# Row normalization on one core: ten-row tiles in five buffers, one whole-row descriptor per partition for each load and store, and two rows of each tile scaled on ScalarE

## The chip, the core and the metric

The kernel runs on one core of a Trainium2 chip. The metric is device time in microseconds (us): the median of 3 runs of the kernel before is 316.5 us (316.41 to 316.51).

## The reference

The input is a 32 x 512 x 1024 array in float32, 67.11 MB. Each row of 1024 values is divided by the sum of its absolute values:

```python
sums = np.sum(np.abs(x), axis=-1, keepdims=True)
return (x / (sums + 1e-8)).astype(np.float32)
```

Every value is read once and written once, 134.22 MB in all.

## The kernel before

The 16384 rows are spread over 128 partitions, 128 rows for each. A tile holds 12 rows per partition, 48 KB per partition and 6 MB in all; the last tile has 8. There are eleven tiles and four buffers (`BUFS = 4`). `piece` says which rows a tile takes: the first 32 rows of every partition (`HEAD`) form one block, which tiles 0, 1 and the last share, so that a partition's rows of these tiles lie in runs inside a block of 128 KB per partition; every other tile is one contiguous block with 48 KB per partition.

`load` (line 87) issues the load of a tile on SyncE's DMA queue, and `store` (line 97) the store on ScalarE's. `max_dma_last_dim` limits the bytes of one descriptor, that is of one contiguous run: `WHOLE` allows 48 KB (a partition's whole share of a tile is one run), `HALF` cuts it into two of 24 KB. Tiles 0 and 1 are loaded with 48 KB runs, all others in halves. The first tile is stored in two DMAs: its first three rows (`FIRST`) as runs of 4 KB, the other nine as runs of 36 KB. The third tile from the end is stored in two DMAs of six rows each; the last two are stored with whole runs; the others in halves. A DMA over 128 partitions is served by 16 DMA engines, 8 partitions on each.

`normalize` computes in place. VectorE sums the absolute values of all rows of the tile in one instruction (line 47), adds the small constant (line 54), takes the reciprocals (line 56) and multiplies most rows by them in one instruction (line 58). `split` names, for some tiles, how many rows go another way: `kt` rows are scaled on VectorE one at a time (line 65), `ks` rows on ScalarE one at a time (line 68). Before, ScalarE scales 4 rows of the first tile, 3 of the next two, 2 of the next to last and 4 of the last, 16 in all.

The order of instructions on each engine is the order of the program (a schedule by hand): four loads first, then for each tile its computation, its store, and the load of the tile that will use its buffer. SyncE's queue therefore holds a load until the store of the buffer's earlier tile has landed, and ScalarE's queue holds its own rows of each tile and then the tile's store.

Of the kernel before, what the change touches and what calls it, by code (L numbers as in the profile page):

```python
# [1 line left out]

# [4 lines left out]

FP32 = mybir.dt.float32
EPS = 1e-8


@with_exitstack
def kernel(
    ctx: ExitStack,
    tc: tile.TileContext,
    x: bass.AP,
    out: bass.AP,
):
    nc = tc.nc
    P = nc.NUM_PARTITIONS  # L20

    x_flat = x.flatten_outer_dims()
    out_flat = out.flatten_outer_dims()
    n, d = x_flat.shape

    R = 12
    BUFS = 4
    HEAD = 32
    per_partition = n // P
    assert n % P == 0 and (per_partition - HEAD) % R == 0  # L30
    rows = [R] * ((per_partition - HEAD) // R + 2) + [HEAD - 2 * R]

    def piece(flat, i):
        head = flat[: P * HEAD, :].rearrange("(p r) d -> p r d", p=P)
        if i < 2:
            return head[:, R * i : R * (i + 1), :]
        if i == len(rows) - 1:
            return head[:, 2 * R :, :]
        a = P * (HEAD + R * (i - 2))
        return flat[a : a + P * R, :].rearrange("(p r) d -> p r d", p=P)  # L40

    sbuf = ctx.enter_context(tc.tile_pool(name="sbuf", bufs=BUFS))
    stats = ctx.enter_context(tc.tile_pool(name="stats", bufs=len(rows)))

    def normalize(x_tile, k, kv, kt):
        s = stats.tile([P, R], FP32)
        nc.vector.tensor_reduce(  # L47
            out=s[:, :k],
            in_=x_tile[:, :k, :],
            axis=mybir.AxisListType.X,  # L50
            op=mybir.AluOpType.add,
            apply_absolute_value=True,
        )
        nc.vector.tensor_scalar_add(out=s[:, :k], in0=s[:, :k], scalar1=EPS)  # L54
        inv = stats.tile([P, R], FP32)
        nc.vector.reciprocal(out=inv[:, :k], in_=s[:, :k])  # L56
        if kv:
            nc.vector.tensor_mul(  # L58
                out=x_tile[:, :kv, :],
                in0=x_tile[:, :kv, :],  # L60
                in1=inv[:, :kv].unsqueeze(2).to_broadcast([P, kv, d]),
            )
        for r in range(kv, kv + kt):
            row = x_tile[:, r, :]
            nc.vector.tensor_scalar_mul(out=row, in0=row, scalar1=inv[:, r : r + 1])  # L65
        for r in range(kv + kt, k):
            row = x_tile[:, r, :]
            nc.scalar.activation(  # L68
                out=row,
                in_=row,  # L70
                func=mybir.ActivationFunctionType.Copy,
                scale=inv[:, r : r + 1],
            )

    last = len(rows) - 1
    split = {0: (3, 4), 1: (0, 3), 2: (0, 3), last - 1: (0, 2), last: (4, 4)}

    tiles = {}

    HALF, WHOLE = 24576, 49152
    FIRST = 3

    def load(i):
        x_tile = tiles[i] = sbuf.tile([P, R, d], FP32, name="x_tile")
        nc.sync.dma_start(out=x_tile[:, : rows[i], :], in_=piece(x_flat, i), max_dma_last_dim=WHOLE if i < 2 else HALF)  # L87

    def store(i):
        if i == 0:  # L90
            parts = [(0, FIRST, 4 * d), (FIRST, R, WHOLE)]
        elif i == last - 2:
            parts = [(0, R // 2, HALF), (R // 2, R, HALF)]
        else:
            parts = [(0, rows[i], WHOLE if i >= last - 1 else HALF)]
        for a, b, size in parts:
            nc.scalar.dma_start(
                out=piece(out_flat, i)[:, a:b, :],
                in_=tiles[i][:, a:b, :],
                max_dma_last_dim=size,  # L100
            )

    def compute(i):
        k = rows[i]
        kt, ks = split.get(i, (0, 0))
        normalize(tiles[i], k, k - kt - ks, kt)

    with tc.manual_schedule():
        for i in range(BUFS):
            load(i)  # L110
        for i in range(len(rows)):
            compute(i)
            store(i)
            if i + BUFS < len(rows):
                load(i + BUFS)


# [1 line left out]
_INS = ['x']  # L119
_OUTS = [((32, 512, 1024), 'float32')]  # L120


# [23 lines left out]
```

## Time and profile before

| What | Value |
|---|---|
| Median of 3 runs | 316.5 us (316.41 to 316.51) |
| Profiled execution: span from first to last instruction | 315.2 us |
| Profiled execution: time of its own beside the span | not listed; the runs lie 1.3 us above the span |
| VectorE (DVE) busy | 260.6 us, 83% of the span, 50 instructions |
| ScalarE (ACT) busy | 18.5 us, 6%, 17 instructions |
| Loads (queue q1) | 11 DMAs, 2736 packets, 67.11 MB |
| Stores (queue q10) | 13 DMAs, 3024 packets, 67.11 MB |
| Mean rate over the span | 426 GB/s |

The page cuts the span into 40 equal slices of 7.9 us. A digit is the busy share of a slice in tenths, 9 meaning 90% or more; for the DMA row it is the mean over the core's 16 DMA engines. Names such as `x_tile<-in_x_dram` are out<-in, and L47 is line 47 of the kernel. DVE is VectorE, ACT is ScalarE, SPq and ACTq are the sequencers of SyncE and ScalarE, which issue DMAs. In the chain and the timeline the first number is the start in us from the start of the span, the second the duration. A packet record in the trace is one descriptor: its queue, its start, its duration and its bytes; the small records of 4 bytes are the semaphore updates that each of the 16 engines makes at the end of a DMA.

### The profile page before, as it was taken

How to read it: one execution, taken by the hardware profiler on the slowest of the kernel's cores; microseconds unless marked ns; L12 is line 12 of the kernel's file. 1: busy time of each engine (PE TensorE's matmuls, PEld its weight loads, DVE VectorE, ACT ScalarE, POOL GpSimd, SP SyncE). 2: the span in 40 equal slices, each digit the busy share in tenths (PEclk: the TensorE clock that was granted, in tenths of full speed). 3: DMA queues.
4: the chain of work that ended last, by engine and by line, in shares of the span. 5: the costliest groups of instructions: out<-in, count | busy, mean ns of one | idle time of the engine just before them, and what ended most of it. 6: DMA issues, size and time to landing. Idle time of an engine off the chain costs nothing.

```text
span 315.2 us, 172 instructions
## 1 busy us (share of the span) xinstructions
DVE 260.6 (83%) x50; ACT 18.5 (6%) x17; POOL 0.2 (0%) x4
## 2 busy tenths in 40 slices
DVE  0079999999999999989996997999699969999000
ACT  0010503004000000000000000000000000203200
POOL 0000000000000000000000000000000000000000
DMA  8999999999999999999999999999999999999997
GB/s 318 480 399 412 437 407 464 411 436 413 415 446 437 415 446 437 415 449 434 415 449 437 412 449 437 412 449 437 415 446 437 415 437 434 432 428 496 399 408 324
DMA packets 5761, 134.22 MB, mean 426 GB/s; under 512 B 385, under 2 KB 385, under 8 KB 769
## 3 DMA queue, kind: packets, MB, share of 16 engines
q1 hardware_dynamic: 2736, 67.11, 49.8%
q10 hardware_dynamic: 3024, 67.11, 49.4%
q14 instruction: 1, 0.00, 0.0%
HBM read 67.11 MB, written 67.11 MB: 426 GB/s over the span
## 4 chain that ended last, share of the span: by engine, by line
DVE 40%; DMA 33%; another core or an unknown queue 18%; ACT 1%; issue 0%; SPq 0%
DVE s L47 23%; DMA x_tile<-in_x_dram 17%; DMA out_dram<-x_tile 16%; DVE x_tile L58 15%; ACT x_tile L68 1%; DVE x_tile L65 1%; DVE inv L56 0%; DVE s L54 0%; SPq L87 0%
## 5 line engine op out<-in xcount | busy, mean ns | idle before, releaser
L47 DVE TENSOR_REDUCE s<-x_tile 128x12 f32<-128x12288 f32 (+1 forms) x11 | 138.2, 12562 | 29.8 <-DMA x_tile<-in_x_dram 29.8
L58 DVE TENSOR_TENSOR x_tile<-x_tile,inv 128x12288 f32<-128x12288 f32 (+3 forms) x10 | 113.6, 11358 | 0.5
L68 ACT ACTIVATE x_tile<-x_tile,inv 128x1024 f32<-128x1024 f32 x16 | 17.2, 1138 | 256.9 <-DVE inv L56 256.9
L65 DVE TENSOR_SCALAR x_tile<-x_tile,inv 128x1024 f32<-128x1024 f32 x7 | 4.8, 749 | 0.0
L56 DVE RECIPROCAL inv<-s 128x12 f32<-128x12 f32 (+1 forms) x11 | 2.5, 226 | 0.4
L68 ACT ACT_TABLE_LOAD x1 | 1.3, 1283 | 17.8 <-DMA x_tile<-in_x_dram 17.8
L54 DVE TENSOR_SCALAR s<-s 128x12 f32<-128x12 f32 (+1 forms) x11 | 1.9, 174 | 0.4
L130 POOL MEMSET const-bfloat16-1.0<- 128x1 bf16 x1 | 0.1, 101 | 0.0
L130 POOL MEMSET const-uint8-127<- 128x1 uint8 x1 | 0.1, 101 | 0.0
L130 POOL MEMSET const-float32-0.0<- 128x1 f32 x1 | 0.1, 98 | 0.2 <-issue 0.2
L130 POOL MEMSET const-float32-1.0<- 128x1 f32 x1 | 0.1, 98 | 0.0
## 6 DMA issues: line engine op xcount, KB each, us to landing
x_tile<-in_x_dram SPq DMA_DIRECT2D x10, 6144.0 KB, 36.9
out_dram<-x_tile ACTq DMA_DIRECT2D x8, 6144.0 KB, 49.1
out_dram<-x_tile ACTq DMA_DIRECT2D x2, 3072.0 KB, 33.4
out_dram<-x_tile ACTq DMA_DIRECT2D x1, 4608.0 KB, 37.9
x_tile<-in_x_dram SPq DMA_DIRECT2D x1, 4096.0 KB, 32.2
out_dram<-x_tile ACTq DMA_DIRECT2D x1, 4096.0 KB, 20.9
out_dram<-x_tile ACTq DMA_DIRECT2D x1, 1536.0 KB, 29.3
```

The lines of the kernel that those rows point to most:

```text
L47: nc.vector.tensor_reduce(out=s[:, :k], in_=x_tile[:, :k, :], axis=mybir.AxisListType.X, op=mybir.AluOpType.add, apply_absolute_value=True,)
L54: nc.vector.tensor_scalar_add(out=s[:, :k], in0=s[:, :k], scalar1=EPS)
L56: nc.vector.reciprocal(out=inv[:, :k], in_=s[:, :k])
L58: nc.vector.tensor_mul(out=x_tile[:, :kv, :], in0=x_tile[:, :kv, :], in1=inv[:, :kv].unsqueeze(2).to_broadcast([P, kv, d]),)
L65: nc.vector.tensor_scalar_mul(out=row, in0=row, scalar1=inv[:, r : r + 1])
L68: nc.scalar.activation(out=row, in_=row, func=mybir.ActivationFunctionType.Copy, scale=inv[:, r : r + 1],)
L130: nc = _bacc.Bacc("TRN2", target_bir_lowering=False, num_devices=1)
```

## The change

A tile has ten rows per partition instead of twelve (40 KB per partition, 5 MB in all), and there are five buffers instead of four. The 128 rows of a partition make twelve tiles of ten rows and a last one of eight, thirteen in all. Every tile is one contiguous block; no block is shared. Each tile is loaded by one DMA and stored by one DMA without a limit on the run, so that a partition's share is one descriptor of 40 KB (32 KB for the last tile). ScalarE scales two rows of every tile, and four of the first and the last, as before in those two. The pool of the small statistics tiles has 26 buffers instead of 11.

```diff
-    R = 12
-    BUFS = 4
-    HEAD = 32
+    R = 10
+    BUFS = 5
     per_partition = n // P
-    assert n % P == 0 and (per_partition - HEAD) % R == 0
-    rows = [R] * ((per_partition - HEAD) // R + 2) + [HEAD - 2 * R]
+    assert n % P == 0
+    rows = [R] * (per_partition // R) + [per_partition % R]
 
     def piece(flat, i):
-        head = flat[: P * HEAD, :].rearrange("(p r) d -> p r d", p=P)
-        if i < 2:
-            return head[:, R * i : R * (i + 1), :]
-        if i == len(rows) - 1:
-            return head[:, 2 * R :, :]
-        a = P * (HEAD + R * (i - 2))
-        return flat[a : a + P * R, :].rearrange("(p r) d -> p r d", p=P)
+        a = P * R * i
+        return flat[a : a + P * rows[i], :].rearrange("(p r) d -> p r d", p=P)
...
-    stats = ctx.enter_context(tc.tile_pool(name="stats", bufs=len(rows)))
+    stats = ctx.enter_context(tc.tile_pool(name="stats", bufs=2 * len(rows)))
...
-    split = {0: (3, 4), 1: (0, 3), 2: (0, 3), last - 1: (0, 2), last: (4, 4)}
+    split = {0: (3, 4), last: (4, 4)}
...
-    HALF, WHOLE = 24576, 49152
-    FIRST = 3
-
     def load(i):
         x_tile = tiles[i] = sbuf.tile([P, R, d], FP32, name="x_tile")
-        nc.sync.dma_start(out=x_tile[:, : rows[i], :], in_=piece(x_flat, i), max_dma_last_dim=WHOLE if i < 2 else HALF)
+        nc.sync.dma_start(out=x_tile[:, : rows[i], :], in_=piece(x_flat, i))
 
     def store(i):
-        if i == 0:
-            parts = [(0, FIRST, 4 * d), (FIRST, R, WHOLE)]
-        elif i == last - 2:
-            parts = [(0, R // 2, HALF), (R // 2, R, HALF)]
-        else:
-            parts = [(0, rows[i], WHOLE if i >= last - 1 else HALF)]
-        for a, b, size in parts:
-            nc.scalar.dma_start(
-                out=piece(out_flat, i)[:, a:b, :],
-                in_=tiles[i][:, a:b, :],
-                max_dma_last_dim=size,
-            )
+        nc.scalar.dma_start(out=piece(out_flat, i), in_=tiles[i][:, : rows[i], :])
 
     def compute(i):
         k = rows[i]
-        kt, ks = split.get(i, (0, 0))
+        kt, ks = split.get(i, (0, 2))
         normalize(tiles[i], k, k - kt - ks, kt)
```

## The prediction

> **What bounds the kernel now.** I read the 40 slices first, then the queues, then the waits of the engines and of the DMA queue, then stretches and the tail of the chain. The 40 slices of the page (busy tenths; 9 is 90% or more):
>
> ```profile
> DVE  0079999999999999989996997999699969999000
> DMA  8999999999999999999999999999999999999997
> GB/s 318 480 399 412 437 407 464 411 436 413 415 446 437 415 446 437 415 449 434 415 449 437 412 449 437 412 449 437 415 446 437 415 437 434 432 428 496 399 408 324
> DMA packets 5761, 134.22 MB, mean 426 GB/s; under 512 B 385, under 2 KB 385, under 8 KB 769
> ```
>
> The DMA row has no hole between its first and last slice. VectorE is also dense, but it has holes, and what it waits for is the loads; ScalarE waits for VectorE, and SyncE's queue for the stores (columns: us in total, times, longest):
>
> ```profile
> ACT x_tile L68 <- DVE inv L56: 256.9, 5, 190.5
> DVE s L47 <- DMA x_tile<-in_x_dram: 29.8, 6, 17.8
> SPq L87 <- DMA out_dram<-x_tile: 242.1, 8, 63.3
> ```
>
> Stretches of the trace (us; busy time of DVE, ACT and POOL; clock; DMA share; GB/s) give the plateau and one dip:
>
> ```profile
> 60.00:65.00 5.00, 5.00 (x2) 0.00 (x0) 0.00 (x0) 1.00 1.01 387
> 90.00:250.00 160.00, 149.89 (x24) 0.00 (x0) 0.00 (x0) 1.00 1.00 433
> ```
>
> So the DMA engines set the end: share 1.00, 433 GB/s for 160 us. In the trace's packet records the first data packet starts at 1.73 us and the last ends at 313.83 us; between them each engine goes from packet to packet. Outside lie 1.7 us ahead and 1.3 us behind. The time is the sum of what each DMA engine pays per descriptor, as long as a queue has something for it.
>
> **What one descriptor costs.** The records have a size and a duration: 4 KB 159 ns, 24 KB 912 ns, 48 KB 1815 ns, alike for loads and stores. From 24 to 48 KB is 903 ns for 24 KB, which leaves 9 ns a descriptor. Successive records overlap: on one engine 48 KB packets start 1812 ns apart, and in the steady stretch SyncE issues a load every 29.08 us:
>
> ```profile
> 160.35 0.37 SPq L87
> ...
> 189.48 0.37 SPq L87
> ...
> 218.50 36.97 DMA x_tile<-in_x_dram
> ```
>
> One 12-row tile in and one out is 32 descriptors of 24 KB per engine: 29.08 / 32 = 909 ns. So a descriptor costs 903 ns per 24 KB and a fixed 6 ns by starts, 9 ns by records. I take 6, since starts make the elapsed time.
>
> **Descriptors before.** Each of 16 engines serves 8 partitions. Loads: 2 tiles x 8, then 8 x 16, then 16 for the last, 160. Stores: 24 + 8 for the first tile, 7 x 16, 2 x 8 (two halves), 8, 8, 176. That is 336; 336 x 16 + 24 DMAs x 16 semaphore records + 1 = 5761, the page's packets. **After:** 13 loads and 13 stores x 8 = 208. The removal of 128 is worth 128 x 6 ns = 0.77 us (9 ns: 1.15; nothing hidden: 0 is the other end). Checked as a sum: before 310.24 us (16 x 1812, 128 x 909, 16 x 608; stores 24 x 156.5, 8 x 1360.5, 128 x 909, 8 x 1210, 8 x 1812), after 192 x 1511 + 16 x 1210 = 309.47. The observed 312.1 us is 310.24 and: 0.74 for first packets (2.25 to 2.85 us where later ones take 1.815), 0.69 for slow 24 KB loads, 0.2 for semaphore records, 0.2 for spread between engines. The first packets stay. Two more DMAs add 2 x 9 ns of semaphore records.
>
> The **slow loads** are the dip at 60 to 65 us: one round of 16 loads took 1.15 to 1.60 us instead of 0.912, and some near 38 to 46 us a little more. Both fall where 24 KB loads alternate with the 4 KB store descriptors of the first tile; over the 160 us in which both sides have 24 KB there are none. The changed kernel has equal sizes from the first store on. No row shows 40 KB beside 40 KB: bounds are all 0.69 gone, and one such round more (+0.6). I take half gone, -0.35, since an accident cannot be told from a pattern with one instance.
>
> **What costs nothing, and its cover.** VectorE: by shape, 12949 ns for 12 rows and 8686 for 8 is 1066 ns a row to reduce; 10825 for ten rows and 9758 for nine is 1067 a row to scale. A middle tile is 10.82 + 0.4 + 8.69 = 19.9 us. DMA needs 2 x 8 x 1511 = 24.2 us for the same tile, so 4.2 us cover it; VectorE's sum falls from 260.6 to about 248 and is not seen. ScalarE gets 30 rows instead of 16 (1138 ns each); two take 2.3 us beside VectorE's 8.7. The store on ScalarE's queue waits for both engines, and behind it stands only the next tile's ScalarE rows, which wait for VectorE anyway. A fifth buffer and thirteen tiles: SyncE issues five loads at the start (26 MB, 60 us of DMA at 433); load 5 waits for store 0. That store is issued near 15 + 10.8 + 0.4 + 5.6 = 32 us and shares the engines until about 57, when loads 3 and 4 are still queued. Without that cover a queue would stand dry for the 1.0 us seen from issue (0.73) to first packet (1.73). More stats buffers take no time; SyncE and ScalarE issue 26 DMAs instead of 24 at about 0.37 us, beside the transfers.
>
> **The tail** must be worked out, for only it can open a hole. From about 34 us both queues are never empty, and the engines take descriptors in turn (in the records of 59 to 62 us, one load of 24 KB and one store of 4 KB alternate; from 255 to 275 us loads of 16 KB beside stores of 24 KB get 0.40 of the bytes, which is 16/40). Equal sizes give halves. By 34 us loads have moved (34 - 2.5) x 433 = 13.6 MB; the other 53.5 at 216 GB/s take 247 us: the last load lands near 282 to 284 us. The last tile is the same 8 rows as now:
>
> ```profile
> 279.79 8.70 DVE s L47
> ...
> 292.09 1.13 ACT x_tile L68
> ```
>
> From landing (279.77) to the store's issue (293.25) is 13.5 us, so the last store comes at 297 us. Then stores have moved 53.5 MB of 67.1 at 283; of 13.6 left, 9.4 to 8.4 MB precede the last, 19 to 22 us, to 302.7. Cover: about 5 us, less 1.0 for issue to first packet. Now it is 304 - 293; the change halves it but leaves it.
>
> **Sum:** -0.77 - 0.35 + 0.02 = -1.1 us. The span 315.2 becomes 314.1. The median of the runs, 316.5, lies 1.3 above the span (the profiled execution has no separate time beside the span); that rest is start and end, unchanged: **315.4 us**.
>
> **Rivals.** A measurement can tell about 0.2%, 0.63 us, from no change.
> 1. *Descriptors cost less than their start-to-start distance says*, and the slow round was chance: gain 0 to 0.6, middle 0.4 (3 ns each), 316.1. For it: 6 ns rests on two large differences. Against: records (9) and starts (6) agree in sign. A 0.6 us slow round eating the gain ends in the same place. Chance 0.24. The Trainium skill, page DMA: Bandwidth & Descriptors, section Why small descriptors are slow, gives a fixed overhead of about 3 cycles a packet against one per 32 bytes. As an estimate by that page, a 24 KB descriptor is 768 + 3 cycles and 128 fewer give 0.45 us, 316.05; the trace's 6 ns is nearly twice its 3.5.
> 2. *The tail runs dry, slower.* Place: between the next-to-last and the last store. If loads got less than half of the turns, the last load lands later and its store is due when no other is left. Share 0.49 shifts the landing by 5 us and spends the cover; 0.486 is the point from which the kernel is slower by 0.2%; 0.48 gives 53.5 / 208 = 257 us instead of 247, 10 late, 5 us of idle engines, 320.4. Against it: the shares of 0.40 above are exactly by size. Chance 0.06.
> 3. *Each DMA has a fixed cost that shows*: 1.0 us from issue to first packet and 0.4 from last packet to landing (313.83 to 314.18), for two more DMAs 2.8 us, 318.2. Against: in 160 us with ten such ends the share stays 1.00. The Trainium skill's same page, section Anatomy of one DMA, fits about 2.0 us fixed per DMA for GpSimd's path; by that estimate 4.0 us, were it serial, which the share of 1.00 speaks against. With it I count a slow round recurring at 40 KB each few tiles, 0.6 each, from four on. Chance 0.08.
> 4. *The runs are split anyway* into two of 20 KB: 416 descriptors, 80 more, +0.5 us, 317.0. The built program has 128x10240 in each transfer, one run. Chance 0.02.
>
> **How the numbers follow.** Forecast 0.60: 314.8 (all 0.69 and 9 ns) to 315.8. Rival 1, 0.24: 315.9 to 316.5, up to 317.0 with a slow round or two. Rivals 2 to 4, 0.16, mostly above 317. Faster 0.61, same 0.24, slower 0.15. The range 314.7 to 317.0 takes in the forecast and rival 1 and leaves out most of the rest.
>
> **What would show it.** Packets 208 x 16 + 26 x 16 + 1 = 3745; a 40 KB record near 1514 ns; loads and stores each 24.2 us apart in the middle; no dip near 60 us; VectorE near 248 us with larger waits for loads (about 32 us after its start); last load near 283, last store issued near 297, store before it done near 303. A DMA slice under 9 before the end, or a record well over 1514 ns, would make the prediction wrong.

## The result: slower by 0.6%

The changed kernel takes 318.5 us (median of 4 runs, 318.23 to 318.89) against 316.5 us before (316.41 to 316.66): a ratio of 1.0062, 95% interval 1.005 to 1.0074. The forecast was 315.4 and its range ended at 317.0. The profiled execution took 318.23 us with a span of 316.5; the rest outside the span is 1.7 to 1.8 us, and 1.6 to 1.7 in runs of the kernel before. A later set of six runs of the same changed kernel ran from 317.1 to 319.0 (median 317.8, ratio 1.0045, 1.0028 to 1.0062). That scatter is part of the result: the kernel before stays within 0.5 us everywhere.

The 40 slices, packets and queues of the page after:

```profile
DVE  0099999999989949949949959958968977979400
DMA  8999999999999999999999999999999999999995
GB/s 326 419 461 445 331 440 456 425 419 414 476 430 419 414 456 450 414 419 445 456 419 419 435 456 430 419 414 476 430 414 419 456 450 429 403 441 425 440 439 236
DMA packets 3746, 134.24 MB, mean 424 GB/s; under 512 B 416, under 2 KB 416, under 8 KB 416
...
q1 hardware_dynamic: 1872, 67.11, 49.7%
q10 hardware_dynamic: 1872, 67.11, 49.0%
q14 instruction: 2, 0.02, 0.0%
```

The packets are those foretold (3744 on the two queues, of which 416 are semaphore records, and two instruction fetches where one was counted on). VectorE has the holes foretold. The DMA row still has no hole, but two slices differ: the fifth moves 331 GB/s, and the last 236 at a busy share of 5 tenths. What VectorE waits for, and the tail of the chain:

```profile
DVE s L41 <- DMA x_tile<-in_x_dram: 47.9, 10, 16.1
```

```profile
284.75 8.70 DVE s L41
...
297.04 1.13 ACT x_tile L62
```

Of the 47.9 us, 31.8 come after the first load (32 foretold); the last load lands at 284.7 and the last store is issued at 298.2 (282 to 284, and 297, foretold). Computing, order and tail went as worked out. The loss is inside the DMA. Stretches of the trace of the changed kernel (DMA share and GB/s stand last):

```profile
34.00:40.00 6.00, 6.00 (x1) 0.00 (x0) 0.00 (x0) 1.00 1.04 362
...
90.00:250.00 160.00, 133.13 (x28) 13.15 (x13) 0.00 (x0) 1.00 1.00 432
...
312.00:313.90 1.90, 0.00 (x0) 0.00 (x0) 0.00 (x0) 1.00 0.48 207
313.90:315.20 1.30, 0.00 (x0) 0.00 (x0) 0.00 (x0) 1.00 0.06 25
```

and of the kernel before:

```profile
312.00:313.90 1.90, 0.00 (x0) 0.00 (x0) 0.00 (x0) 1.00 0.64 276
313.90:315.20 1.30, 0.00 (x0) 0.00 (x0) 0.00 (x0) 1.00 0.00 0
```

Two things are to be seen. Between 34 and 40 us the engines are as busy as ever and move 362 GB/s instead of 433. The share there is no guard: a slow packet counts as busy. Single loads take up to 3.56 us where 1.51 is usual, which is the prediction's own sign of being wrong (a record well over 1514 ns). And from 313.9 to 315.2 us the share is 0.06, which is one packet in progress on one of 16 engines; before, the engines had all ended by then.

### The profile page after: what moved, and what is told of

The parts are those of the page before. It is cut to its first block, busy times and chain, and to the rows that moved or that the text cites. A ratio compares the mean times of both kernels' runs of the same rounds, so it can differ in the third digit from the quotient of the medians.

```text
span 316.5 us, 209 instructions
## 1 busy us (share of the span) xinstructions
DVE 247.0 (78%) x58; ACT 33.9 (11%) x31; POOL 0.2 (0%) x4
## 4 chain that ended last, share of the span: by engine, by line
DVE 77%; another core or an unknown queue 10%; DMA 5%; ACT 1%; issue 1%; DVEq 0%
DVE s L41 44%; DVE x_tile L52 31%; DMA x_tile<-in_x_dram 5%; ACT x_tile L62 1%; DVE inv L50 1%; DVE s L48 1%; DVE x_tile L59 1%; DVEq L52 0%
## 5 line engine op out<-in xcount | busy, mean ns | idle before, releaser
L41 DVE TENSOR_REDUCE s<-x_tile 128x10 f32<-128x10240 f32 (+1 forms) x13 | 138.5, 10653 | 47.9 <-DMA x_tile<-in_x_dram 47.9
L52 DVE TENSOR_TENSOR x_tile<-x_tile,inv 128x8192 f32<-128x8192 f32 (+1 forms) x12 | 99.0, 8248 | 0.8
L62 ACT ACTIVATE x_tile<-x_tile,inv 128x1024 f32<-128x1024 f32 x30 | 32.6, 1139 | 248.1 <-DVE inv L50 248.1
L50 DVE RECIPROCAL inv<-s 128x10 f32<-128x10 f32 (+1 forms) x13 | 2.8, 216 | 0.4
L48 DVE TENSOR_SCALAR s<-s 128x10 f32<-128x10 f32 (+1 forms) x13 | 2.2, 173 | 0.4
```

The costliest lines, as they stand in the source:

```text
L41: nc.vector.tensor_reduce(out=s[:, :k], in_=x_tile[:, :k, :], axis=mybir.AxisListType.X, op=mybir.AluOpType.add, apply_absolute_value=True,)
L52: nc.vector.tensor_mul(out=x_tile[:, :kv, :], in0=x_tile[:, :kv, :], in1=inv[:, :kv].unsqueeze(2).to_broadcast([P, kv, d]),)
L62: nc.scalar.activation(out=row, in_=row, func=mybir.ActivationFunctionType.Copy, scale=inv[:, r : r + 1],)
```

## Reading the packets engine by engine

Each engine ends a DMA with its own semaphore record, so the last 16 records of the store queue are the ends of the 16 engines. And each packet record can be held against the usual duration of its size; the sum of what is over, as a mean per engine, is called the excess here. First packets (before 3 us) are left out of it; they cost 0.6 to 0.9 us in every kernel. The excess is nearly all on loads (the most on stores in this table is 0.3, in d1). A packet record does not name its engine. Where the text speaks of one engine, its packets were put in a chain: each packet behind the one that ends where it starts, within some ns, and with gaps of up to 0.8 us for a few loads in the burst near 36 us. So what is said of single engines is worked out, not read off.

| Kernel | Descriptors per engine | Excess of loads, us per engine | Mean end of the 16 engines | Last engine's end | Median us (lowest to highest) |
|---|---|---|---|---|---|
| before | 336 | 0.68 | 313.5 | 313.8 | 316.5 (316.4 to 316.7) |
| changed | 208 | 1.33 | 313.6 | 315.2 | 318.5 (318.2 to 318.9) |
| d0: changed, again | 208 | 1.35 | 313.6 | 315.8 | 317.8 (317.1 to 319.0) |
| a4: without ScalarE's rows | 208 | 1.28 | 313.5 | 314.4 | 318.8 (317.5 to 319.5) |
| c3: shared block | 208 | 1.45 | 313.8 | 314.6 | 317.5 (317.3 to 318.9) |
| a1: 4 KB first rows | 232 | 1.42 | 313.9 | 315.4 | 318.7 (318.1 to 321.2) |
| d1: block and 4 KB | 232 | 1.20 | 313.9 | 315.4 | 318.0 (317.4 to 318.5) |
| e2: 20 KB at the start | 272 | 1.10 | 313.8 | 315.7 | 318.2 (317.4 to 318.7) |
| a2: 20 KB | 416 | 0.91 | 314.3 | 315.0 | 318.0 (317.9 to 318.1) |
| a3: 20 KB, 4 KB first | 432 | 0.83 | 314.2 | 315.1 | 318.1 (318.0 to 318.2) |
| d2: 20 KB, block | 416 | 0.94 | 314.3 | 314.9 | 317.9 (317.9 to 318.2) |
| d3: 20 KB, block, 4 KB | 432 | 0.99 | 314.3 | 314.9 | 318.0 (317.9 to 318.1) |
| c1: a2 with shorter programs | 416 | 0.97 | 314.2 | 314.7 | 318.1 (317.9 to 318.8) |
| b1: before, first store whole | 312 | 1.23 | 313.9 | 314.1 | 317.5 (317.1 to 317.7) |
| b2: before, 48 KB | 208 | 1.13 | 313.4 | 316.0 | 318.8 (316.5 to 319.4) |
| b4: before, 12 KB in the first store | 352 | 0.57 | 313.4 | 313.7 | 316.6 (316.5 to 316.8) |
| c2: before, contiguous | 336 | 0.76 | 313.6 | 314.8 | 317.4 (317.1 to 317.8) |
| e1: before, 16 KB | 472 | 0.66 | 314.1 | 314.5 | 317.9 (317.4 to 318.3) |

Excess and ends are those of the one profiled run, the medians those of 5 to 11 runs (4 for the first two rows). The profiled run can be any of them: in a4 it is the fastest (317.46 us), in d0 one of the slowest (318.89). The kernel before beside them had medians of 316.5 to 316.6.

In the 19 profiled runs with a time of their own (all kernels here but the one before), the time is 2.9 to 3.3 us more than the last engine's end, and 3.1 to 10.5 us more than the mean end. So the time follows the last engine.

## The experiments

The theory that the trace suggested first was **J**: when the first store of long descriptors joins engines that are full of loads, the loads slow down once (34 to 40 us here), more than with the 4 KB rows of the kernel before, and unequally. The rival **S**: long descriptors as such let single engines fall behind, at any time. Further theories are named where they arise: **L** (layout of the first loads), **F** (instruction fetches).

**a1, the first store's 4 KB rows put back:**

```diff
+        parts = [(0, 3, 4 * d), (3, R, 49152)] if i == 0 else [(0, rows[i], 49152)]
...
```

> The changed kernel, with the first store as in the kernel before: its first three rows in runs of 4 KB, the other seven in one run of 28 KB. Theory J (joining: loads slow down once when the first store of large descriptors enters engines full of loads, and the engine hit worst sets the end): the slow loads near 34 to 40 us shrink from 1.3 us per engine to at most 0.8, the engines end within 0.7 us of each other, and the time falls by 0.8 to 1.5 us to about 317.0 to 317.7. Rival S (40 KB descriptors as such let the engines drift): no change, 318.2 to 318.9, last engine still 1 us behind. Rival O (what lies outside the span, 1.8 us against 1.35 before, comes from more instructions): that rest stays at 1.8 under either.

Measured 318.7 us (ratio 1.0089, 1.0063 to 1.0116), up to 321.2 in one run. The slow loads at 34 to 40 us are gone (0.07 us of excess up to 50 us), but others come, at 65, at 81 to 94 and here and there until 271 us. In the stretch of 80 to 95 us of this run:

```profile
80.00:95.00 15.00, 14.90 (x5) 2.19 (x2) 0.00 (x0) 1.00 1.02 415
```

The share is full and the rate is 415 instead of 433. J describes the first burst rightly but not the time, which is what S expects (its last engine is 1.5 us behind the mean).

**a2, all runs halved to 20 KB:**

```diff
-        nc.sync.dma_start(out=x_tile[:, : rows[i], :], in_=piece(x_flat, i))
+        nc.sync.dma_start(out=x_tile[:, : rows[i], :], in_=piece(x_flat, i), max_dma_last_dim=2 * rows[i] * d)
```

(the same in `store`)

> The changed kernel with every descriptor cut in two, 20 KB instead of 40 KB (416 per engine instead of 208). By the price of 6 ns a descriptor it costs 208 x 6 = 1.25 us more. Theory J: the first store still joins with large descriptors, so the slow loads stay, perhaps about half of 1.3 us per engine since the descriptor that joins is half as long; net between +0.3 and +1.3, 318.8 to 319.8. Rival S (40 KB as such): the spread between engines falls under 0.7 us and the time falls to about 317.5 or less.

Measured 318.0 us, and all five runs within 0.14 us. The mean end is 0.7 us later (twice as many descriptors, and 0.4 us less of slow loads), yet the time is no higher, since the last engine is 0.7 us behind the mean instead of 1.6. Neither expectation is met whole: slow loads stay at 35 to 38 us, as J has it, and the scatter goes, as S has it, but the time lies between the two.

**b1, the first store of the kernel before in one piece:**

```diff
-            parts = [(0, FIRST, 4 * d), (FIRST, R, WHOLE)]
+            parts = [(0, R, WHOLE)]
```

> The kernel before with its first store as one DMA of 48 KB runs, nothing else changed. Theory J: the loss now appears in the kernel before: slow loads of about 1.0 to 1.5 us per engine within 5 us of the first store's issue instead of 0.7 in all, unequal engines, time up by 0.5 to 2 us to 317.0 to 318.5. Rival S or O: 316.5 less the price of 24 descriptors (0.14 us), about 316.3 to 316.5.

Measured 317.5 us (1.0027, 1.0016 to 1.0038), with 24 descriptors fewer. The stretch after the store's issue at 38.8 us:

```profile
38.00:44.00 6.00, 6.00 (x3) 0.00 (x0) 0.00 (x0) 1.00 1.14 410
```

The excess rises from 0.68 to 1.23 us per engine, all of it before 44 us, and the mean end by 0.4. The engines stay within 0.5 us of each other. J is a real cost, of about what the changed kernel's excess shows, but here it makes no engine late. The remainder of the 0.9 us lies outside the span (2.0 us instead of 1.6 to 1.7).

**b2, 48 KB runs in the kernel before** (by count 128 fewer descriptors, 208 left; the expectation's first number is a slip):

```diff
-    HALF, WHOLE = 24576, 49152
+    HALF, WHOLE = 49152, 49152
```

> The kernel before with 48 KB runs everywhere except the first three rows stored and the two half stores of the third tile from the end, which keep 4 and 24 KB; 168 fewer descriptors... of 336 an engine has 208. Theory J: the first store still joins with 4 KB, so the descriptors' price shows: 128 x 6 ns = -0.8 us, 315.5 to 316.3. Rival S (large descriptors as such): slower than 316.5, 317.5 to 318.5, with engines ending over 1 us apart.

Measured 318.8 us (1.006, 1.0037 to 1.0083), from 316.5 to 319.4. The mean end is the lowest of all (313.4), the last engine 2.6 us behind it. One run of the six took 316.5 us, as the kernel before does. In its last stretch:

```profile
312.00:313.90 1.90, 0.00 (x0) 0.00 (x0) 0.00 (x0) 1.00 0.24 104
313.90:315.20 1.30, 0.00 (x0) 0.00 (x0) 0.00 (x0) 1.00 0.12 50
```

Here tile size, buffers, layout, first rows and ScalarE's share are those of before: long descriptors alone make engines drift, in most runs. The spread between the engines grows from 0.6 us at 100 us to 3.4 at 280. This is S.

**a3, both cures in the changed kernel:**

```diff
+        parts = [(0, 3, 4 * d), (3, R, 49152)] if i == 0 else [(0, rows[i], 2 * rows[i] * d)]
...
```

(and loads in runs of 20 KB)

> The changed kernel with both cures together: first store's three rows in runs of 4 KB (its other seven in one run of 28 KB), all other transfers in runs of 20 KB. Theory JS (two separate losses: a large first store joining the loads costs 0.8 to 1.2 us on every engine once, and long descriptors let loads slow down here and there on single engines all through, so that one engine ends late): slow loads at 20 to 50 us fall under 0.2 us per engine, none later beyond 0.6 in all, ends within 0.9 us; against the 20 KB kernel (318.0) 0.4 to 0.8 less, 317.2 to 317.6. Rival J alone: the same. Rival S alone: 318.0.

Measured 318.05 us, as a2, where 317.2 to 317.6 was expected. The slow loads leave 34 to 40 us and come back at 54 to 56 us (0.67 us per engine), near the end of the 4 KB runs: 4 KB rows postpone the loss, as in the kernel before, where it stands at 62 us.

The packet records say more of the moment. The burst of slow loads lies just ahead of the first store packet longer than 4 KB, wherever that stands: 34.1 to 37.8 us with that packet at 38.4 in the changed kernel, 39.1 to 42.7 and 43.6 in b1, 54.1 to 56.4 and 56.2 in a3, 62.3 to 64.2 and 65.0 in the kernel before, and 57.2 to 58.8 and 58.7 in e1 (below). It does not follow the issue of the second store, which comes at 61.8 us in e1. So loads are slow shortly before the long runs begin, not while the two alternate; the records do not show why.

**a4, without ScalarE's two rows:**

```diff
-        kt, ks = split.get(i, (0, 2))
+        kt, ks = split.get(i, (0, 0))
```

> The changed kernel without the two ScalarE rows of the eleven middle tiles (VectorE scales all ten). VectorE then needs 10.8 + 0.4 + 10.7 = 21.9 us a tile against 24.2 of DMA, so nothing of it is on the path: by JS the time stays at 318.2 to 318.9, with the same slow loads at the first store and one engine a microsecond late. If ScalarE's beside VectorE's traffic or the two instruction fetches that fall into the run (near 267 and 280 us, 0.3 us on one engine each) had a part in the late engine, one or both fetches disappear and the time falls by up to 0.5 us.

Measured 318.8 us, 317.5 to 319.5: no gain, and as much scatter. One of the two instruction fetches, near 267 us, falls out of the run. ScalarE's share has no part in the loss that shows.

**a6 and a7, unequal runs:** loads of 20 KB beside stores of 40, and the reverse (the edit of a2 in `load` alone, or in `store` alone).

> The changed kernel with loads in runs of 20 KB and stores in runs of 40 KB. Engines take descriptors in turn, so loads get a third of the bytes while stores wait: this tries the tail of the prediction's second rival. Last load near 291 us instead of 284, last store issued near 306, with holes in the DMA of about 3 us near 291 and 1.3 near 306: by this the time is 4 to 5 us over the changed kernel, 322 to 324. JS: slow loads and spread as with 20 KB, since it is loads that slow down. If turns were not by descriptor the last load would stay near 284 and the time within 1 us of 318.5.

> The changed kernel with loads in runs of 40 KB and stores in runs of 20 KB: 104 more descriptors per engine, +0.6 us. Loads get two thirds, the last load lands near 262 us and the tail has 30 us of cover. Whether long loads or long stores make the engines drift: if long loads, slow loads appear after 50 us and the ends spread over 1 us, 318.3 to 320; if long stores, the ends lie within 0.8 us and the time is about 317.8 to 318.3, near the 20 KB kernel's.

Both measured 326.4 us (1.0288, 1.0265 to 1.0311; 1.0298, 1.0277 to 1.032). In a6 the tail runs dry, the mechanism of the prediction's second rival:

```profile
DMA  7999999999999999999999999999999999994987
```

```profile
292.00:300.00 8.00, 8.00 (x2) 0.28 (x1) 0.00 (x0) 1.00 0.47 198
300.00:313.00 13.00, 10.55 (x7) 4.27 (x4) 0.00 (x0) 1.00 0.82 353
```

The shares of 0.47 over 8 us and 0.82 over 13 us are about 6.5 us of hole, where 4.3 were expected. Slow packets come on top, 2.6 us per engine on loads and 0.9 on stores against 1.3 in all in the changed kernel. The 16 engines end within 0.2 us of each other. In a7 the tail has its cover, and the time is as long for another reason:

```profile
316.00:323.00 7.00, 0.00 (x0) 0.00 (x0) 0.00 (x0) 1.00 0.06 26
```

For seven microseconds one engine of 16 works through its last stores. From the semaphore records of the stores the last engine is 1.8 us behind the first at 150 us and 16 at the store that the first ends at 261. Loads are slow here and there from 108 us on (1.55 us per engine). Why one engine falls back so far when the two queues carry unequal runs was not settled.

**c1, shorter programs:** a2 without ScalarE's middle rows and without the addition of 1e-8, which is left out.

```diff
-        nc.vector.tensor_scalar_add(out=s[:, :k], in0=s[:, :k], scalar1=EPS)
```

> The changed kernel in runs of 20 KB (318.0), without the ScalarE rows of the middle tiles and without the addition of 1e-8 to the sums, which is left out: 13 VectorE and 22 ScalarE instructions fewer. Theory F (fetches): the two instruction fetches near 267 and 279 us that every ten-row kernel shows hold one DMA engine each for about 0.5 us, and those two engines end last (314.88 and 314.99 where the next is 314.42); with shorter programs both fetches move behind the end, and the time falls by 0.4 to 0.6 to 317.4 to 317.6. If the late engines have another cause, 318.0.

No fetch falls into the run any more (one is seen behind it, at 317.9 us), and the last engine's end falls from 315.0 to 314.7, but the time is 318.1: what lies outside the span grows from 1.8 to about 2.0 us. F falls as a cause of the loss.

**c2 and c3, the layout both ways:**

```diff
+        a = P * R * i
+        return flat[a : a + P * rows[i], :].rearrange("(p r) d -> p r d", p=P)
```

(c2: these lines in the kernel before, in place of those of the shared block; c3, not shown: the shared block's lines, with 28 rows, in the changed kernel)

> The kernel before with contiguous tiles: no shared block of 32 rows, everything else as it was. Theory L (layout of the first loads): the first load's engines finish 0.6 us apart in all kernels with the shared block and 1.0 to 1.3 in all with contiguous tiles, since the last engine starts later (2.6 us instead of 2.1 to 2.4); here that spread grows to 1.0 or more and the time to 316.8 to 317.3. If layout has no part, 316.4 to 316.7.

> The changed kernel with tiles 0, 1 and the last in one shared block of 28 rows per partition (runs of 40 KB as before, pitch 112 KB): the converse. Theory L: the first load's spread falls from 1.3 to about 0.6 and the time by 0.3 to 0.8, to about 317.8; the slow loads near 34 to 40 us stay at 1.2 us per engine. If layout has no part, 318.2 to 318.9.

c2 measured 317.4 us (1.0025, 1.0016 to 1.0034, ten runs), c3 317.5 (1.0037, 1.0024 to 1.0049), both times about as L has it. In c2 the mean end is that of before within 0.1 us, and only the last engine is later, by 1.0; the first load's spread is 1.4 us instead of 0.6. In c3 that spread falls only from 1.3 to 1.1 us, where L expected 0.6, so there L's mechanism is not seen. And the changed kernel's own repeat (d0) has a median of 317.8, so c3's gain cannot be told from the scatter.

**b4, 12 KB instead of 36 KB in the first store's second part:**

```diff
-            parts = [(0, FIRST, 4 * d), (FIRST, R, WHOLE)]
+            parts = [(0, FIRST, 4 * d), (FIRST, R, 3 * 4 * d)]
```

> The kernel before with the second part of its first store (nine rows) in runs of 12 KB instead of 36 KB; 16 more descriptors, +0.1 us. Theory J in doses: the loss of 0.56 us per engine near 62 us, where the 36 KB runs come up in the store queue behind the 4 KB ones, falls to about 0.2, and the next store's 24 KB runs meet no loads (they come at 76 us, when only stores are left); net -0.2 to -0.3, 316.2 to 316.4. If size of the joining store has no part: 316.6 to 316.7.

Measured 316.6 us (1.0003, 0.9994 to 1.0011): no change, where J in doses expected 0.2 to 0.3 less. The burst at 62 us falls from 0.56 to 0.39 us per engine, not to 0.2, and 16 descriptors take 0.1 of the gain.

**d0 to d3, layout, first rows and run length combined** (d1, d2, d3 are a1, a2, a3 with c3's block):

> The changed kernel again, beside the next three. All theories: 318.2 to 318.9; slow loads of about 1.2 us per engine near 34 to 40 us. If the late engine comes from the layout of the first loads (theory L), the spread of the first load is again over 1.0 us and the engine that is last there is among the last at the end.

> The changed kernel with the shared block of 28 rows and the first store's three rows in runs of 4 KB; 40 KB runs stay. Theory LJ (layout and first store are all): 317.5 less 0.6 to 0.9, 316.6 to 316.9. Theory LJS (long runs let the loads slow down now and then wherever the two queues do not carry equal runs from the first store on): slow loads of over 0.5 us per engine after 60 us, times scattered over more than 1 us, median 317.3 or more.

> The changed kernel with the shared block of 28 rows and all runs of 20 KB. LJ: 317.5 plus 1.1 for 208 more descriptors, 318.3 to 318.6. LJS: layout takes 0.9 from the 20 KB kernel's 318.0, 316.9 to 317.2, and the runs lie within 0.3 us.

> The changed kernel with all three undone: shared block, 4 KB first rows, runs of 20 KB; tiles of ten rows, five buffers and ScalarE's two rows stay. LJS: 316.9 to 317.2, what is left over 316.6 being the price of 96 more descriptors than before (0.5 us at 5 to 6 ns) and two instruction fetches. If the tile size or ScalarE's rows cost something of their own, 317.5 or more.

Measured 317.8, 318.0, 317.9 and 318.0 us. In d0 the engine that ends last is the one that ended the first load last; by the chains that is so in the changed kernel's first profile, in a4 and in e2 too, but not in b2. With 20 KB, neither layout nor first rows matter: a2, a3, d2 and d3 lie between 317.9 and 318.1. With 40 KB (changed, d0, c3, a1, a4, d1) medians go from 317.5 to 318.8 and runs from 317.1 to 321.2. L and J, which each cost 0.8 to 0.9 in the kernel before, do not add up in the changed one.

d3 has the layout, the first rows and 20 KB runs, and is still 1.5 us slower than the kernel before; its expectation reads 317.5 or more as a cost of the tile size or of ScalarE's rows. Its trace puts 0.8 us of that in the mean end (96 descriptors more per engine, and 0.3 us more of slow loads), 0.2 in the lag of the last engine and 0.1 outside the span. Whether tiles of ten rows bring the slow loads and the lag was not tested apart.

**e1 and e2:**

```diff
-    HALF, WHOLE = 24576, 49152
+    HALF, WHOLE = 16384, 49152
```

(e1, in the kernel before; e2 is the changed kernel with)

```diff
+        nc.sync.dma_start(out=x_tile[:, : rows[i], :], in_=piece(x_flat, i), max_dma_last_dim=20480 if i < BUFS else 40960)
...
+        nc.scalar.dma_start(out=piece(out_flat, i), in_=tiles[i][:, : rows[i], :], max_dma_last_dim=20480 if i < 3 else 40960)
```

> The kernel before with its half runs of 24 KB cut to 16 KB (12 KB in the two half stores): 472 descriptors per engine instead of 336, nothing else. By the prediction's price 136 x 6 = 0.8 us more, 317.3 to 317.5, with runs within 0.3 us of each other. If the price is hidden: 316.5 to 316.7.

> The changed kernel with runs of 20 KB in loads 0 to 4 and stores 0 to 2, 40 KB from there on: 64 descriptors more per engine, +0.4 us. If the late engine is made in the first 40 us (long runs where loads and the first store meet), the spread between engines stays near that of the 20 KB kernels, the runs lie within 0.5 us, and the time is 316.9 to 317.5, less than the changed kernel's. If long runs make engines late all through, or the change from 20 to 40 KB runs does, the runs scatter over 1 us or more with a median of 317.8 or above, and slow loads appear after 80 us.

e1 measured 317.9 us (1.004, 1.0028 to 1.0053) with a scatter of 0.8 us; the mean end is later by 0.65 us where 0.8 were expected. The price of a descriptor is real, at about 5 ns. The profiled run is the fastest of the five, 317.4, with the last engine 0.3 us behind the mean; the rest, up to 318.3, have no trace. So scatter is not confined to long runs, and what makes it here is open. e2 measured 318.2 us, 317.4 to 318.7, with slow loads again at 189 to 273 us and one engine 1.9 us behind the mean. By the chains, 1.4 us of slow loads after 100 us fall on that engine, where the mean is 0.15. So the late engine is not made in the first 40 us alone.

## Why the prediction was wrong, by its own steps

- **Descriptors, -0.77 us:** right. Usual durations summed over an engine's packets, less 3 ns of overlap each, fall from 310.45 to 309.71 us, -0.74; a 40 KB record takes 1514 ns as foretold. By time the price is seen in e1, and in b2 the mean end is 0.1 us earlier in spite of 0.45 us more of slow loads.
- **Slow loads, half gone, -0.35:** wrong in sign. The excess went from 0.68 to 1.33 us per engine, +0.65; the stated upper bound was +0.6. This takes back nearly all of the gain: the mean end of the engines is 313.6 against 313.5. The step laid the round at 62 us to 24 KB loads alternating with 4 KB rows, and half to accident. b1, a3 and d3 show that it comes with the first long store run, once in every kernel here, whatever stands ahead of that run. It costs 1.0 to 1.4 us per engine with 40 or 48 KB in the first store, 0.8 to 0.9 with 20 KB, and 0.2 to 0.8 with 4 KB rows ahead.
- **"0.2 for spread between engines", unchanged:** this is the step that failed most. The sum was made for one engine and taken for all. The time goes by the last engine, and its lag behind the mean rose from 0.3 us to 1.6 (2.2 in d0). By the chains the lag adds up: in the changed kernel the last engine started at 2.63 us (mean 1.97), had 1.02 us over in its first packets (mean 0.66), 1.90 in the burst (mean 1.24) and a little after it. 0.66 + 0.36 + 0.66 = 1.7, and it ends 1.6 late. So 1.0 us of it is there when the first load ends and the rest when the burst does; after 42 us the engines of this run keep their distance (the loads' spread is 2.4 us at 42 us and 2.6 at 282), unlike those of b2, d0 and e2. Nothing takes work off a late engine: each moves 104 loads and 104 stores. The Trainium skill, DMA: Bandwidth & Descriptors, section iDMA fabric, remarks, beside an explanation that it calls unconfirmed, that a bulk load runs at the pace of its slowest engine; this trace agrees, 315.2 us against a mean of 313.6.
- **The rest outside the span, 1.3 us, unchanged:** the 1.3 set the profiled span against other runs' times; by each run's own span the rest is 1.6 to 1.7 us before and 1.7 to 1.8 now, 0.1 more. Mean end +0.1, lag +1.3 and this +0.1 make 1.5 of the 1.7 us by which the profiled run is above 316.5.
- **Why nothing in the profile of before said so:** its engines end within 0.6 us of each other, with 24 KB runs on both sides and no slow load after 64 us. The worst 40 KB load after the change took 3.56 us, 2.05 over; the worst 24 KB load before was 0.69 over.
- **Tail, cover and VectorE:** right, as above; a6 shows that the rival on the tail was well placed, but equal runs kept it away. The first store's first packet came 5.5 us after its issue, not 1.0 (3.8 in the kernel before), while loads filled the engines.
- **Rivals:** a slow round coming back every few tiles, counted at 0.08 with others, is nearest in time, but in the changed kernel's own trace slow loads do not come back (0.06 us per engine after 80 us). They do in a1, at 83 to 94 us, and in d1, at 82 to 86 and 116 to 123. No rival has one late engine.

What is settled: the long descriptors' saving is there, the slow loads ahead of the first long store take as much back, and the end is set by a late engine, which long runs alone (b2) can bring about. What is open: why single loads are slow, why engines drift in some runs with 40 and 48 KB, why e1 scatters with 16, and how much of the changed kernel's 2 us belongs to the layout or to the tile size. No version here beats the kernel before: b4 equals it.

## What to carry to other kernels

Where DMA is saturated, sum the packets of the last engine, not of the mean one, and look at how far the 16 ends lie apart before crediting a saving below 1 us. Longer descriptors save some 5 to 6 ns each and were paid for here with slow loads and a late engine; in the kernel before, with runs of 24 KB on both queues for most of the time, the engines stayed together. In this schedule unequal runs on the two queues were dear: a factor of two cost 8 us against the changed kernel in either direction, once by a dry tail and once by one late engine.

## What the runs showed of the hardware

A DMA share of 1.00 can hide a loss: the share was 1.04 while 362 GB/s moved instead of 433. While both queues have work, engines take turns by descriptor, so run lengths set the shares of bandwidth: in a7 the 40 KB loads get 0.63 of the bytes beside 20 KB stores between 40 and 58 us, and in a6 the 20 KB loads 0.37 beside 40 KB stores between 46 and 70 us, near the two thirds and one third of their sizes. The end of a saturated transfer is that of its last engine, up to 7.5 us behind the mean (a7). Instruction fetches during the run take a packet of 0.31 us on one engine (two of them in the changed kernel, near 267 and 280 us), and when shorter programs moved them behind the end, the time did not fall.
